# A Strassen-blocked encoder block: where the standard steps stand among a group's phases, shorter leads, and three first sums made by adding transfers

## The chip, the cores and the metric

The kernel runs on one core of a Trainium2 chip. Times are device microseconds (us) of one execution of the whole program; a kernel's time is the median of its runs. One further execution is taken with the hardware profiler, and all rows shown here come from it. The engines are called as the profile calls them: PE (matrix multiplies), DVE (vector), ACT (scalar and activation), POOL (GpSimd) and SP, which here only issues transfers; transfers issued by SP and by POOL go through the core's 16 DMA engines.

## What is computed

One encoder block on 256 frames of 2048 values, all in float32: a half-step SwiGLU feed-forward network, then attention and retention side by side with gates, then a second half-step feed-forward network and a norm.

```python
def swiglu_ffn(x, w_gate, w_up, w_down):
    return (jax.nn.silu(x @ w_gate) * (x @ w_up)) @ w_down
...
x = x + 0.5 * swiglu_ffn(rmsnorm(x, norm_ffn1_g[l]), ffn1_w_gate[l], ffn1_w_up[l], ffn1_w_down[l])
...
x = x + 0.5 * swiglu_ffn(rmsnorm(x, norm_ffn2_g[l]), ffn2_w_gate[l], ffn2_w_up[l], ffn2_w_down[l])
```

`w_gate` and `w_up` are 2048 x 5632, `w_down` is 5632 x 2048. The change touches these two networks alone (named f1 and f2 below); the mixing part between them has the same work in the same order.

## The kernel before

**Products.** Each float32 product is made of three passes: a weight tile `raw` (256 rows x 512 columns, 512 KB, held as 128 x 1024) is split into `hi` by a cast on ACT (L128) and `lo = raw - hi` by a subtraction on DVE (L129), and PE multiplies activations hi with weights hi (L139), activations lo with weights hi (L140) and activations hi with weights lo (L142). A *standard step* takes one such weight tile and both halves of the frames: 12 matmuls of 512 columns.

**Groups.** The 11 blocks of 512 columns of `w_gate` and `w_up` are, but for block 10 (`plain`, standard steps), taken pairwise: one *group* (class `Strassen`, tiles named `z` and a number) multiplies both weights with a Strassen scheme of 7 products in place of 8. A group has four phases. Its steps have 6 matmuls each; they are called `r` (a weight tile as it is) and `s` (a sum of weight tiles), with phase and tile number: `r00` is phase 0, tile 0; `s03` is phase 0, tile 3. In the profile's names `hiz8403s` is the hi part of s03 of group z84. The order in a group is r00 r01 s00 r02 s01 r03 s02 s03, then the same for phases 1 and 2, then s30 to s33: 28 steps. Each network has ten groups.

- Phase 0 needs per tile number a tile `k` of `w_up` and a tile `x` of `w_gate`, loaded by POOL's queue (L542), and the *first sum* x + k. For tiles 0 and 1 DVE makes it (`first`, L531); for tiles 2 and 3 (`ADDED`) POOL issues a transfer that loads `w_up` once more and adds it onto x on the way (L546, `accum_op=ALU.add`). Such a transfer can't be issued before x has landed, and what stands behind it on POOL's queue waits with it.
- Phase 1 loads `raw` tiles by SP; each r step is followed by an addition to x (L593), each s step by k = x - k on DVE (L579) and an adding transfer onto x by POOL (L580, called the *third sum* below).
- Phase 2 loads `raw` tiles by SP and uses k; phase 3 uses x. When the last third sum has been issued, POOL's queue goes on to the loads of the next group's k and x.

Phases 0 (s) and 1 (r) accumulate in one bank, `c`: after s03, ACT takes the sum out (L636), and r10 then writes the bank anew.

**Weaving.** `weave` writes the program's steps in order: a *lead* of standard steps (`LEAD`), then the groups, with standard steps put between pairs of group steps. `SHARE` has 16 numbers, one for each pair of phases 0 to 2 and each single step of phase 3; a standard step is put in when the summed share, times a rate, passes a threshold (lower at a phase's end), and in any case at the end of phase 2. The standard steps are those of block 10, then those of `w_down` for blocks that are ready; each two of the latter are a job whose bank ACT fills and empties (L785, L788). `HELD` and `apart` keep a number of them for the end.

**Look-ahead.** `run` writes, for step c, the splits of up to step c + 3 ahead of c's matmuls (`SPLIT_BUFS` = 4 pairs of hi and lo). So ACT and DVE can be at most four steps ahead of PE, and the cast of a step waits until PE has read the hi of the step four before. SP has 5 `raw` tiles. `kept` are the loads of k and x: for the first group of a network they start 8 steps ahead of the group.

Of the kernel before, what the change touches and what calls it, by code (L numbers as in the profile page):

```python
# [11 lines left out]
ALU = mybir.AluOpType  # L12
# [6 lines left out]
D = 2048  # L19
# [7 lines left out]
NB = 512  # L27
KC = 2
# [7 lines left out]
TAIL = 4  # L36
AHEAD = (2, 3)
HALF_K = D // P // 2
LEAD = 12
MIX_LEAD = 8  # L40
RET_WAIT = (14, 5)
HELD = 6

MIX_SHARE = (0.85,) * 4 + (1.0,) * 4 + (0.8,) + (0.4,) * 3 + (0.15,) * 4
SHARE = (0.7,) * 2 + (0.2,) * 2 + (1.3,) * 4 + (0.3,) * 4 + (0.2,) * 4
ADDED = (2, 3)
PLAIN = 10
PASSES = ((10,),) + tuple((b,) for b in range(10))
GATE_WAIT = 5
# [25 lines left out]
def block_kernel(ctx: ExitStack, tc: tile.TileContext, x, g1, w1g, w1u, w1d, gm, w_in, rel, woa, wor, wo,  # L75
                 g2, w2g, w2u, w2d, gf, cos, sin, decay, ident, out):
    nc = tc.nc
# [19 lines left out]
    def tmp_tile(name, tag="t", bufs=None):  # L97
        return tmp.tile([P, NB], F32, tag=tag, name=name, bufs=bufs)


    steps = []
# [6 lines left out]
    def later(n, fn):  # L108
        due.setdefault(state["step"] + n, []).append(fn)
# [4 lines left out]
    def chunk(w, r0, c0):  # L114
        return w[r0 : r0 + KC * P, c0 : c0 + NB].rearrange("(k p) n -> p k n", p=P)
# [399 lines left out]
    class Strassen:  # L515
# [21 lines left out]
        def loads(self):  # L537


            def go(tiles, i, jc):  # L540
                tiles[jc] = apool.tile([P, KC, NB], F32, tag="act", name=f"{self.name}{'kx'[i]}{jc}")
                nc.gpsimd.dma_start(tiles[jc], chunk(self.w[i], self.rows(0, jc), self.col[i]))  # L542

            def add_on():
                for jc in self.added:
                    nc.gpsimd.dma_start(self.x[jc], chunk(self.w[0], self.rows(0, jc), self.col[0]), accum_op=ALU.add)  # L546

            out = [
                lambda tiles=tiles, i=i, jc=jc: go(tiles, i, jc)
                for jc in range(HALF_K // KC) for i, tiles in enumerate((self.kept, self.x))  # L550
            ]
            out[-1] = lambda last=out[-1]: [last(), add_on()]
            return out

        def steps(self):

# [103 lines left out]
    def down_done(b, factor, after):  # L660
        def done(acc):
            for t in range(NT):
                xb = xs[t][:, b * NB : (b + 1) * NB]
                nc.vector.scalar_tensor_tensor(xb, acc[t], factor, xb, op0=ALU.mult, op1=ALU.add)
            if after is not None:
                after(b)

        return done
# [11 lines left out]
    def weave(jobs, apart, groups, lead, share, start=None):  # L680


        queue = [(job, k) for job in jobs for k in range(0, job.nk, KC)]
        at_hand = {}

        def next_standard():

            if len(queue) <= apart:
                return False
            job, k = queue[0]  # L690
            if any(at_hand.get(b, len(steps) + 1) > len(steps) for b in job.needs):
                return False
            steps.append(standard(job, k))
            del queue[0]
            if job.makes is not None and k + KC == job.nk:
                at_hand[job.makes] = len(steps) + 6
            return True

        for _ in range(lead):
            next_standard()  # L700
        rate = (len(queue) - apart) / (len(groups) * sum(share))
        credit = 0.0
        first = len(steps) - 8
        for n, (b, make) in enumerate(groups.items()):
            group = make()
            loads = group.loads()
            if start is not None and n == 0:
                loads[0] = lambda load=loads[0]: [start(), load()]
            kept.extend((first + i if n == 0 else 0, fn) for i, fn in enumerate(loads))
            for i, part in enumerate(group.steps()):  # L710
                steps.extend(part)
                credit += rate * share[i]
                if i + 1 == len(share):
                    at_hand[b] = len(steps) + 7

                turn = i + 1 == 3 * (HALF_K // KC)
                if (turn or credit >= (0.2 if (i + 1) % (HALF_K // KC) == 0 else 0.6)) and next_standard():
                    credit -= 1
        for job, k in queue:
            steps.append(standard(job, k))  # L720

    def ffn(name, norm, wg, wu, wd, after, start=None):


        nblocks = DFF // NB
        mids, ready = {}, {}

        def put_mid(b, hs):
            mids[b] = Operand(f"{name}a{b}", 1)
            for t in range(NT):  # L730
                mids[b].put(0, t, hs[t])

        def plain(b):
            gates = {}

            wait = GATE_WAIT if start is not None and b == PLAIN else 0

            def gate_done(acc):
                def go():
                    for t in range(NT):  # L740
                        gates[t] = tmp_tile(f"{name}g{b}{t}", "gate", 2)
                        nc.scalar.activation(gates[t], acc[t], AF.Silu, scale=norm.scale(t))

                if wait:
                    later(wait, go)
                else:
                    go()

            def up_done(acc):
                for t in range(NT):  # L750
                    a = gates[t]
                    nc.vector.scalar_tensor_tensor(a, acc[t], norm.scale(t), a, op0=ALU.mult, op1=ALU.mult)  # L752
                later(4, lambda: put_mid(b, gates))

            tags = ("acc", "acc")
            up = Gemm(wu, 0, b * NB, D // P, norm, up_done, tags)
            up.makes = b
            return [Gemm(wg, 0, b * NB, D // P, norm, gate_done, ("z", "z") if wait else tags), up]

        def paired(b):  # L760
            got = {}

            def evict(t, side, r):
                if side == 1:
                    nc.scalar.activation(r, r, AF.Silu)
                    got[t] = r
                    return
                nc.vector.scalar_tensor_tensor(got[t], r, norm.scale(t), got[t], op0=ALU.mult, op1=ALU.mult)
                if t == 1:
                    later(4, lambda: put_mid(b, got))  # L770

            return Strassen(norm, wu, b * NB, wg, b * NB, evict, ADDED)

        def down(blocks, last):

            jobs = []

            def act(k, t):
                return mids[blocks[k // 4]](k % 4, t)

            for b in range(D // NB):
                cols = slice(b * NB, (b + 1) * NB)

                def seed(acc, t, cols=cols):
                    nc.scalar.activation(acc, xs[t][:, cols], AF.Copy, scale=2.0)  # L785

                def evict(acc, t, cols=cols):
                    nc.scalar.activation(xs[t][:, cols], acc, AF.Copy, scale=0.5)  # L788

                if last:  # L790
                    job = Gemm(wd, 0, b * NB, 4 * len(blocks), act, down_done(b, 0.5, after))
                else:
                    job = Gemm(wd, 0, b * NB, 4 * len(blocks), act, None, ("acc", "acc"), seed)
                    job.evict = evict
                job.rows = [(m * 4 + i) * P for m in blocks for i in range(4)]
                job.needs = blocks
                jobs.append(job)
            return jobs

        downs = {blocks: down(blocks, blocks is PASSES[-1]) for blocks in PASSES}  # L800
        jobs = plain(PLAIN) + [job for p in PASSES for job in downs[p]]
        for job, follow in zip(jobs, jobs[1:]):
            job.next = follow
        groups = {b: (lambda b=b: paired(b)) for b in range(nblocks) if b != PLAIN}
        weave(jobs, len(downs[PASSES[-1]]) * len(PASSES[-1]) * 4 // KC + HELD, groups, LEAD, SHARE, start)


    n1 = Norm("n1", gains[:, 0, :], True)
# [221 lines left out]
    def gates(col1, col2, func, dsts):  # L1030


        def evict(t, side, r):
            if side == 1:
                nc.scalar.activation(r, r, func)
            else:
                bank, r = r, tmp_tile(f"sg{col1}{t}", "gate", 2)
                nc.scalar.activation(r, bank, func, scale=nm.scale(t))
            nc.scalar.dma_start(dsts[side][:, t, :], r)

        return Strassen(nm, w_in0, col1, w_in0, col2, evict)

    both = ("acc", "acc")
    groups = {
        b: (lambda b=b: gates(GA + b * NB, GG + b * NB, AF.Sigmoid, merge_dram[b])) for b in range(D // NB)
    }
# [219 lines left out]
```

## Time and profile before

| | |
|---|---|
| time, median of 3 runs | 2078.74 us (2076.82 to 2080.69) |
| the profiled execution's own time | 2079.74 us |
| its span, first to last instruction | 2078.0 us |
| PE busy, weight loads busy | 99%, 81% |
| DVE, ACT, POOL busy | 85%, 72%, 16% |
| transfers by SP's queue (q1), by POOL's (q0) | 301.50 MB, 189.44 MB |
| granted PE clock | 0.999 |

A row of a list of groups gives busy time and mean duration, then idle time before and what ended it. A row of a timeline gives start, duration, engine, line, operation, what is written and read, and in brackets the engine's idle time just before and what ended it. Matmuls are pipelined: a 512-column matmul is shown as 0.39 us long while the next one starts 0.23 us after it, so PE is shown busy for 0.16 us of every wait, and a short wait isn't shown as one. PE's idle time is therefore read here from starts and from counts of instructions.

### The profile page before, as it was taken

The page shows a single profiled execution, that of the slowest core. Times are in us where ns is not written, and L with a number is a line of the kernel's source. Part 1 is how long each engine was busy: PE and PEld are TensorE (multiplying, and loading weights), DVE is VectorE, ACT ScalarE, POOL GpSimd, SP SyncE. Part 2 cuts the span into 40 slices and gives each one's busy share as a digit, 9 for nine tenths or more (in the row PEclk, how much of TensorE's full clock was granted, in tenths as well). Part 3 has the DMA queues.
Part 4 walks back from the last instruction along what each step waited for, and adds up shares of the span by engine and source line. Part 5 has one row for each costly group of instructions (what it writes and reads, how often), then busy time and mean ns, then how long its engine had stood idle before and what let it go on. Part 6 is the DMA issues. An engine that isn't in the chain of part 4 may idle for free. (4 is left out here: it accounts for less than half of the span.)

```text
span 2078.0 us, 26280 instructions
## 1 busy us (share of the span) xinstructions
PE 2047.3 (99%) x9208; PEld 1680.7 (81%) x9208; DVE 1768.2 (85%) x1836; ACT 1490.7 (72%) x1892; POOL 342.3 (16%) x386
## 2 busy tenths in 40 slices
PE   9999999999999999999999999999999999999998
PEld 7777888877888888888888888887878888778877
DVE  7898999989998799899966667568889999889996
ACT  8677888777887767776665434556788787778775
POOL 2221222221122110122100000011122222122210
PEclk9999999999999999999999999999999999999999
DMA  9778889887888777798775645577789888889974
GB/s 325 228 211 247 259 264 289 256 236 226 251 261 251 243 206 258 260 289 252 224 271 174 223 144 189 185 253 181 244 255 291 267 237 231 251 251 272 298 208 132
DMA packets 230325, 498.47 MB, mean 240 GB/s; under 512 B 15584, under 2 KB 16336, under 8 KB 230192
## 3 DMA queue, kind: packets, MB, share of 16 engines
q1 hardware_dynamic: 156736, 301.50, 42.9%
q0 software_dynamic: 70112, 189.44, 35.7%
q10 hardware_dynamic: 3344, 5.84, 0.8%
q8 instruction: 72, 1.18, 0.2%
q14 instruction: 61, 0.50, 0.1%
HBM read 487.81 MB, written 8.91 MB: 239 GB/s over the span
## 5 line engine op out<-in xcount | busy, mean ns | idle before, releaser
L129 DVE TENSOR_TENSOR lo<-raw,hi 128x1024 fp32r<-128x1024 f32 x367 | 447.8, 1224 | 163.4 <-ACT hi L128 161.1
L128 ACT CAST hi<-raw 128x1024 fp32r<-128x1024 f32 x367 | 384.0, 1050 | 206.4 <-PE acc L140 140.0
L788 ACT ACTIVATE xall<-acc 128x512 f32<-128x512 f32 x160 | 94.5, 591 | 17.6 <-PE acc L142 13.1
L785 ACT ACTIVATE acc<-xall 128x512 f32<-128x512 f32 x160 | 95.8, 599 | 15.2 <-DVE f1g L752 7.0
L139 PE MATMUL acc<-hi,mgh 128*128 128x512 f32 x128 | 50.2, 392 | 0.0
L140 PE MATMUL acc<-hi,mgl 128*128 128x512 f32 x128 | 49.8, 389 | 0.0
L139 PE MATMUL acc<-hi,nma01h 128*128 128x512 f32 x96 | 38.6, 403 | 0.0
L139 PE MATMUL acc<-hi,nma00h 128*128 128x512 f32 x96 | 38.6, 402 | 0.0
L140 PE MATMUL acc<-hi,nma00l 128*128 128x512 f32 x96 | 37.5, 390 | 0.0
L139 PE MATMUL acc<-hi,nma10h 128*128 128x512 f32 x96 | 37.5, 390 | 0.0
L140 PE MATMUL acc<-hi,nma01l 128*128 128x512 f32 x96 | 37.5, 390 | 0.0
L140 PE MATMUL acc<-hi,nma11l 128*128 128x512 f32 x96 | 37.4, 390 | 0.0
L139 PE MATMUL acc<-hi,nma11h 128*128 128x512 f32 x96 | 37.4, 390 | 0.0
L140 PE MATMUL acc<-hi,nma10l 128*128 128x512 f32 x96 | 37.4, 390 | 0.0
L142 PE MATMUL acc<-lo,mgh 128*128 128x512 f32 x128 | 35.5, 389 | 0.0
L142 PE MATMUL acc<-lo,nma01h 128*128 128x512 f32 x96 | 29.6, 390 | 0.0
L142 PE MATMUL acc<-lo,nma00h 128*128 128x512 f32 x96 | 29.6, 389 | 0.0
L142 PE MATMUL acc<-lo,nma11h 128*128 128x512 f32 x96 | 29.6, 389 | 0.0
L142 PE MATMUL acc<-lo,nma10h 128*128 128x512 f32 x96 | 29.6, 389 | 0.0
L142 PEld LDWEIGHTS acc<-lo,mgh 128*128 128x128 f32 x128 | 24.0, 188 | 5.0
L140 PEld LDWEIGHTS acc<-hi,mgl 128*128 128x128 f32 x128 | 24.0, 188 | 4.9
L139 PEld LDWEIGHTS acc<-hi,mgh 128*128 128x128 f32 x128 | 24.0, 188 | 4.8
(6634 smaller groups left out, 7144.1 us busy)
## 6 DMA issues: line engine op xcount, KB each, us to landing
raw<-in_ffn_w_down_dram SPq DMA_DIRECT2D x176, 512.0 KB, 6.6
raw<-in_w_in_dram SPq DMA_DIRECT2D x96, 512.0 KB, 4.7
raw<-in_w_out_dram SPq DMA_DIRECT2D x32, 512.0 KB, 4.4
raw<-in_ffn_w_up_dram SPq DMA_DIRECT2D x16, 512.0 KB, 10.3
raw<-in_w_out_att_dram SPq DMA_DIRECT2D x16, 512.0 KB, 4.2
raw<-in_w_out_ret_dram SPq DMA_DIRECT2D x16, 512.0 KB, 4.1
raw<-in_ffn_w_gate_dram SPq DMA_DIRECT2D x15, 512.0 KB, 5.1
z392x<-in_w_in_dram POOLq DMA_DIRECT2D x8, 512.0 KB, 7.5
```

Of the source, the lines that this page charges most:

```text
L128: nc.scalar.copy(hi, raw)
L129: nc.vector.tensor_sub(lo, raw, hi.bitcast(F32))
L139: nc.tensor.matmul(acc, ahi, whi, start=first, stop=False, **more)
L140: nc.tensor.matmul(acc, alo, whi, start=False, stop=False, **more)
L142: nc.tensor.matmul(acc, ahi, wlo, start=False, stop=last, **more)
L785: nc.scalar.activation(acc, xs[t][:, cols], AF.Copy, scale=2.0)
L788: nc.scalar.activation(xs[t][:, cols], acc, AF.Copy, scale=0.5)
```

## The change

Four things change, all in the two feed-forward networks:

- `SHARE` has large numbers in phases 0 and 1, zero in phase 2. The number of standard steps stays the same.
- The lead is 10 standard steps in f1 and 8 in f2, in place of 12. The first group's loads are not staged ahead of step 4.
- First sums 1, 2 and 3 are adding transfers; DVE makes number 0 alone.
- The adding transfer of tile n is issued right behind the load of x of tile n + 1, and that of tile 3 last, where before both stood behind all loads.

```diff
-LEAD = 12
+LEAD = (10, 8)
...
-SHARE = (0.7,) * 2 + (0.2,) * 2 + (1.3,) * 4 + (0.3,) * 4 + (0.2,) * 4
-ADDED = (2, 3)
+SHARE = (0.75,) * 4 + (1.0,) * 4 + (0.0,) * 4 + (0.2,) * 4
+ADDED = (1, 2, 3)
...
-            def add_on():
-                for jc in self.added:
-                    nc.gpsimd.dma_start(self.x[jc], chunk(self.w[0], self.rows(0, jc), self.col[0]), accum_op=ALU.add)
-
-            out = [
-                lambda tiles=tiles, i=i, jc=jc: go(tiles, i, jc)
-                for jc in range(HALF_K // KC) for i, tiles in enumerate((self.kept, self.x))
+            def add_on(jc):
+                nc.gpsimd.dma_start(self.x[jc], chunk(self.w[0], self.rows(0, jc), self.col[0]), accum_op=ALU.add)
+
+            def both(jc):
+                go(self.x, 1, jc)
+                if jc - 1 in self.added:
+                    add_on(jc - 1)
+                if jc + 1 == HALF_K // KC and jc in self.added:
+                    add_on(jc)
+
+            return [
+                (lambda jc=jc: both(jc)) if i else (lambda jc=jc: go(self.kept, 0, jc))
+                for jc in range(HALF_K // KC) for i in range(2)
             ]
-            out[-1] = lambda last=out[-1]: [last(), add_on()]
-            return out
...
-        first = len(steps) - 8
+        first = max(len(steps) - 8, D // NB)
...
-        weave(jobs, len(downs[PASSES[-1]]) * len(PASSES[-1]) * 4 // KC + HELD, groups, LEAD, SHARE, start)
+        weave(jobs, len(downs[PASSES[-1]]) * len(PASSES[-1]) * 4 // KC + HELD, groups, LEAD[start is None], SHARE, start)
```

Written out, the order of a middle group, with `+` for a standard step, goes from (z191) `r00 r01 + s00 r02 s01 r03 s02 s03 + r10 r11 + s10 r12 + s11 r13 + s12 s13 + r20 r21 s20 r22 s21 r23 + s22 s23 + s30 s31 s32 s33`, or (z120) `r00 r01 s00 r02 + s01 r03 s02 s03 r10 r11 + s10 r12 + s11 r13 + s12 s13 + r20 r21 + s20 r22 s21 r23 s22 s23 + s30 s31 s32 s33 +`, to the same in all groups of f1 but the first: `r00 r01 + s00 r02 s01 r03 + s02 s03 + r10 r11 + s10 r12 + s11 r13 + s12 s13 + r20 r21 s20 r22 s21 r23 s22 s23 + s30 s31 s32 s33`. In f2 some groups have `r00 r01 s00 r02 + s01 r03 + s02 s03 +` in its place.

On PE, at the end of phase 0 of the third group of f1 (named z84 before and z82 now; the number is that of the step at which the group begins), this stood before:

```order
L140 MATMUL z84c_1641<-hiz8403s_1690,n1s5l_291 128x512
L139 MATMUL z84c_1641<-hiz8403s_1690,n1s5h_290 128x512
L140 MATMUL z84c_1641<-hiz8403s_1690,n1s5l_291 128x512
L142 MATMUL z84c_1641<-loz8403s_1691,n1s5h_290 128x512 x2
L139 MATMUL z84c_1641<-hiz8410r_1700,n1s3h_474 128x512
L140 MATMUL z84c_1641<-hiz8410r_1700,n1s3l_475 128x512
```

Here s03's last product is followed at once by r10's first, in the same bank. At the same place now:

```order
L142 MATMUL z82c_1615<-loz8203s_1661,n1s5h_290 128x512 x2
L139 MATMUL acc14_0_1690<-hi92_1672,f1a0h0_1098 128x512
L140 MATMUL acc14_0_1690<-hi92_1672,f1a0l0_1099 128x512
L139 MATMUL acc14_0_1690<-hi92_1672,f1a0h0_1098 128x512
L140 MATMUL acc14_0_1690<-hi92_1672,f1a0l0_1099 128x512
L142 MATMUL acc14_0_1690<-lo92_1673,f1a0h0_1098 128x512 x2
L139 MATMUL acc15_1_1693<-hi92_1672,f1a0h0_1098 128x512
L140 MATMUL acc15_1_1693<-hi92_1672,f1a0l0_1099 128x512
L139 MATMUL acc15_1_1693<-hi92_1672,f1a0h0_1098 128x512
L140 MATMUL acc15_1_1693<-hi92_1672,f1a0l0_1099 128x512
L142 MATMUL acc15_1_1693<-lo92_1673,f1a0h0_1098 128x512 x2
L139 MATMUL z82c_1615<-hiz8210r_1696,n1s3h_473 128x512
```

A whole standard step of `w_down` (banks acc) has moved between the two.

On POOL, the loads and adding transfers of the fifth group's first sums (z156 before) stood like this; `k0` is tile 0 of k:

```order
L542 DMA z156k0_2458<-in_ffn1_w_up_dram 128x2x512
L542 DMA z156x0_2484<-in_ffn1_w_gate_dram 128x2x512
L542 DMA z156k1_2520<-in_ffn1_w_up_dram 128x2x512
L542 DMA z156x1_2532<-in_ffn1_w_gate_dram 128x2x512
L542 DMA z156k2_2556<-in_ffn1_w_up_dram 128x2x512
L542 DMA z156x2_2568<-in_ffn1_w_gate_dram 128x2x512
L542 DMA z156k3_2583<-in_ffn1_w_up_dram 128x2x512
L542 DMA z156x3_2601<-in_ffn1_w_gate_dram 128x2x512
L546 DMA z156x2_2568<-in_ffn1_w_up_dram 128x2x512
L546 DMA z156x3_2601<-in_ffn1_w_up_dram 128x2x512
```

And now (the same group is z154, the adding transfers are L545):

```order
L542 DMA z154k0_2440<-in_ffn1_w_up_dram 128x2x512
L542 DMA z154x0_2471<-in_ffn1_w_gate_dram 128x2x512
L542 DMA z154k1_2496<-in_ffn1_w_up_dram 128x2x512
L542 DMA z154x1_2508<-in_ffn1_w_gate_dram 128x2x512
L542 DMA z154k2_2532<-in_ffn1_w_up_dram 128x2x512
L542 DMA z154x2_2544<-in_ffn1_w_gate_dram 128x2x512
L545 DMA z154x1_2508<-in_ffn1_w_up_dram 128x2x512
L542 DMA z154k3_2560<-in_ffn1_w_up_dram 128x2x512
L542 DMA z154x3_2584<-in_ffn1_w_gate_dram 128x2x512
L545 DMA z154x2_2544<-in_ffn1_w_up_dram 128x2x512
L545 DMA z154x3_2584<-in_ffn1_w_up_dram 128x2x512
```

There is one adding transfer more, and k3 and x3 now stand behind the first of them, which waits for x1.

## The prediction

> **What bounds the kernel now.** I read the page's busy times first, then PE's waits, then windows of whole groups, and last the timelines of POOL, DVE and ACT over one group.
>
> ```profile
> PE 2047.3 (99%) x9208; PEld 1680.7 (81%) x9208; DVE 1768.2 (85%) x1836; ACT 1490.7 (72%) x1892; POOL 342.3 (16%) x386
> ```
>
> PE is the bound, and the change leaves its matmuls as they are. So only PE's waits can come or go. By name they are small (total, times, longest):
>
> ```profile
> PE z84c L139 <- ACT z84s L636: 0.8, 1, 0.8
> PE z263c L142 <- DVE loz26300s L129: 0.6, 1, 0.6
> ```
>
> Since ends of matmuls are modelled, waits are better counted. The next rows are stretches of the two networks: us, then busy time and count of PE, PEld, DVE, ACT, POOL, then PE clock, DMA share, GB/s.
>
> ```profile
> 110.90:274.60 163.70, 160.47 (x710) 130.18 (x709) 152.37 (x140) 127.49 (x157) 35.04 (x39) 1.00 0.83 237
> 274.60:396.00 121.40, 121.40 (x545) 100.72 (x544) 113.01 (x105) 98.69 (x121) 25.57 (x29) 1.00 0.89 259
> 396.00:640.00 244.00, 239.97 (x1063) 195.66 (x1063) 221.38 (x204) 191.33 (x233) 49.10 (x53) 1.00 0.86 252
> 1412.40:1447.50 35.10, 34.57 (x154) 27.73 (x153) 31.04 (x29) 21.71 (x25) 3.58 (x3) 1.00 0.60 156
> 1447.50:2007.00 559.50, 551.92 (x2443) 450.23 (x2442) 512.30 (x472) 442.47 (x540) 120.91 (x131) 1.00 0.87 255
> ```
>
> The second stretch, two groups long, has PE busy without a gap: 121.40 / 545 = 0.2228 us per PE instruction row. At that pitch the others would take 158.2, 236.8, 34.3 and 544.2 us. They took 5.5, 7.2, 0.8 and 15.3 us more: **28.8 us of waits**, the most that the new placing can win there. The clock is 1.00 throughout. A group at full pitch takes 60.7 us (two in 121.4).
>
> What nearly bounds as well is a loop through POOL. This is POOL in group z191, in the stretch without a gap (start, duration, idle before):
>
> ```profile
> 332.82 1.23 POOL L542 DMA_DIRECT2D z191k<-in_ffn_w_up_dram  x1
> 337.19 1.20 POOL L542 DMA_DIRECT2D z191k<-in_ffn_w_up_dram  x1
> 342.04 0.73 POOL L542 DMA_DIRECT2D z191x<-in_ffn_w_gate_dram  x1 [3.65 <-issue]
> 354.88 1.23 POOL L546 DMA_DIRECT2D z191x<-in_ffn_w_up_dram  x1 [12.11 <-DMA z191x<-in_ffn_w_gate_dram]
> 359.04 1.21 POOL L546 DMA_DIRECT2D z191x<-in_ffn_w_up_dram  x1 [2.93 <-DVE z191x L531]
> 392.82 1.19 POOL L580 DMA_DIRECT2D z191x<-in_ffn_w_up_dram  x1 [1.09 <-ACT hiz19120r L128]
> 393.55 1.23 POOL L542 DMA_DIRECT2D z227k<-in_ffn_w_up_dram  x1
> ```
>
> And ACT's cast of s03, which needs the last adding transfer, with DVE from there to the last addition of phase 1:
>
> ```profile
> 366.74 1.05 ACT L128 CAST hiz19103s<-z191x 128x1024 fp32r<-128x1024 f32 x1 [0.58 <-DVE loz19102s L129]
> 367.82 1.22 DVE L129 TENSOR_TENSOR loz19103s<-z191x,hiz19103s 128x1024 fp32r<-128x1024 f32 x1
> 370.61 1.22 DVE L129 TENSOR_TENSOR loz19110r<-rawz19110r,hiz19110r 128x1024 fp32r<-128x1024 f32 x1 [0.43 <-ACT hiz19110r L128]
> 371.75 1.22 DVE L593 TENSOR_TENSOR z191x<-z191x,rawz19110r 128x1024 f32<-128x1024 f32 x1
> 391.05 1.23 DVE L579 TENSOR_TENSOR z191k<-z191x,z191k 128x1024 f32<-128x1024 f32 x1
> ```
>
> The loop: k0 is issued at 332.82; s03 is cast at 366.74, **33.9 us** later; then DVE works through phase 1 back to back (only the 0.43 us of idle is spare), the last third sum is issued at 392.82, and the next k0 at 393.55. From the cast to there are 26.8 us, without the idle 26.4. Period 60.7: exactly a group of PE's. So a first leg of 60.7 − 26.4 = 34.3 us is free, and z191 uses 33.9. That is possible to use up, because z191 has just three standard steps (8.2 us of PE) between the preceding r20 and s02; so had z156, z335, z840, z875 and z1019, where others had four.
>
> **The change part by part.** *Placing.* Each group now has a standard step between s03 and r10, and phases 1 and 2 as z191 has them, including six steps of phase 2 without a standard one, which cost z191 no wait. PE's waits for ACT L636 (the bank's emptying, now behind 2.72 us of other work) and for the lo of s00 (a standard step now precedes it, as in z191) go. I take 28 of the 28.8 us, leaving 0.8 for stray ones: **−28**. Cover: the standard steps; where it fails, the 0.8 us of the row above comes back at each of 18 boundaries. What becomes late next is the loop above, since by the written order fifteen groups (all but the first two of f1, and z728, z801, z837, z873, z910, z982, z1018 of f2) now have three standard steps before s02.
>
> *Leads.* The first group of f1 loses its start either way:
>
> ```profile
> 44.70:110.90 66.20, 63.02 (x274) 49.83 (x273) 58.35 (x62) 47.49 (x59) 13.81 (x15) 1.00 0.83 238
> ```
>
> 274 rows at 0.2228 are 61.0 us; 5.2 are waits for loads and splits just begun. Ten lead steps leave 5.4 us less time for them and then find more standard steps inside the group; between −5 and +5, I take 0, as PE work and loads both keep their sums. f2's lead likewise.
>
> *First sum 1 by transfer.* DVE loses this, 20 times in all (busy total and mean of one):
>
> ```profile
> L531 DVE TENSOR_TENSOR z191x<-z191x,z191k 128x1024 f32<-128x1024 f32 x2 | 2.4, 1222 | 0.0
> ```
>
> That is 24.4 us of DVE, but in phase 0, where the leg waits for transfers; so no gain on the path. POOL's 20 added issues of 1.2 us are hidden while it waits. The price is paid in the 16 DMA engines: do they have room in the leg?
>
> ```profile
> 340.00:357.00 17.00, 17.00 (x77) 14.08 (x76) 14.32 (x14) 14.40 (x18) 1.96 (x2) 1.00 1.03 388
> 367.00:371.00 4.00, 4.00 (x19) 3.31 (x18) 3.57 (x5) 3.71 (x5) 0.00 (x0) 1.00 0.00 0
> 1976.00:1979.00 3.00, 3.00 (x15) 2.46 (x14) 2.00 (x3) 1.52 (x3) 0.00 (x0) 1.00 1.02 164
> ```
>
> They are full (1.03) while the loads run, at 388 GB/s, and idle only after s03's transfer is in. The last row is a lone adding transfer (of z1019, below): the engines are as full (1.02), but move 164 GB/s. 512 KB (524 thousand bytes) at 164 GB/s take **3.2 us**, against 1.35 at 388. Put into a full leg, that makes 33.9 + 3.2 = 37.1, 2.8 over 34.3.
>
> The Trainium skill ("DMA: Bandwidth & Descriptors", section "Anatomy of one DMA — SWDGE (gpsimd) path") gives one price for each transfer issued by GpSimd, about 2.0 us fixed plus bytes over 436 GB/s; the fixed part being mostly a wait for the write's receipt, the engines would by it be taken for 1.2 us (an estimate), added or plain. The trace's plain loads come near that with 388 GB/s, its adding transfer doesn't.
>
> *The order.* The adding transfer of x1 waits for x1, and k3 and x3 now stand behind it. Issue to landing of the four k tiles:
>
> ```profile
> DMA to landing us min/median/max: 10.4/14.7/19.2
> ```
>
> k0 landed at 343.2 (the least, 10.4) and k3 at 356.4 (the greatest, from 337.19), six tiles later: 2.2 us each, so x1 at 349.8. Half a microsecond more to the transfer's issue, 0.7 for each issue (steps of the rows above): x3 goes out at 351.8, 19 us after k0, where it went at 342.04, 9.2 after. z1019 has this delay by chance, since four transfers of `gf` came between its loads:
>
> ```profile
> 1943.26 1.23 POOL L542 DMA_DIRECT2D z1019k<-in_ffn_w_up_dram  x1
> 1945.46 2.65 POOL L1209 DMA_DIRECT2D gf<-in_norm_final_g_dram  x4
> 1959.82 0.72 POOL L542 DMA_DIRECT2D z1019x<-in_ffn_w_gate_dram  x1 [0.38 <-issue]
> 1974.16 1.21 POOL L546 DMA_DIRECT2D z1019x<-in_ffn_w_up_dram  x1 [3.72 <-DVE z983c L768]
> 1980.15 1.05 ACT L128 CAST hiz101903s<-z1019x 128x1024 fp32r<-128x1024 f32 x1 [0.65 <-DMA z1019x<-in_ffn_w_up_dram]
> ...
> PE z1019c L139 <- ACT hiz101903s L128: 0.5, 1, 0.5
> ```
>
> x3 went out 16.6 us after k0, and s03's cast came at 36.9, waiting for the transfer, with PE behind it. Two estimates agree; I take the seen one, 36.9: **36.9 + 26.4 = 63.3, 2.6 us over a group of PE's**, 14 times = 36.4. Bounds: nothing, if the lost delay and the added bytes fit where other loads give way; and 5.0: x3 sent at 351.8, landing as in z1019 13.9 us later, 0.5 to the issue, 5.9 to the cast there, makes 372.1, a leg of 39.3. In the fifteenth, z1018, `gf` comes as well: 36.9 + 3.2 − 34.3 = 5.8.
>
> Sum: 36.4 + 5.8 − 28 = **+14.2**. The profiled execution took 2079.74 us; that gives 2093.9. The median of the runs is 1.0 lower: **2093 us**.
>
> **The rivals.**
>
> *Hidden transfers (the other side).* The engines' order lets the added transfer through in time: raw tiles of SP, which share the engines and are wanted later than s02 and s03, give way. For it: at 367 the engines go idle, and 0.89 of DMA share over the clean groups leaves 6.7 us per group. Against: the share is full in just the leg that counts, and z1019's wait. It decides where the leg stays under 34.3, that is 0.4 us over z191's. Then −28, and z1018 unharmed: 2051.
>
> *The price of a plain transfer.* If the adding transfer costs what a load costs where others run beside it, the leg is 33.9 + 1.35 = 35.25, 0.95 over: 14 × 0.95 = 13.3, z1018 about 3: −28 + 16 = −12, **2067**. The Trainium skill's single price for both kinds, named above, leads here. For it: the 164 GB/s are those of a transfer with no other beside it. Against: the engines' time was full with it.
>
> *Even.* At 1.7 us a group, 23.8 + 4.9 − 28 is about 0: 2079; 1.4 to 1.9 gives this, between the last one and the forecast.
>
> *Serial.* Each transfer behind x1 waits out the one before, 5.0 per group: 70 + 8.2 − 28 = +50, 2129.
>
> That the change does not do what it says is no case: the written order shows the standard steps behind s03, and the third adding transfer ahead of k3.
>
> **How the numbers follow.** Forecast (1.9 to 3.4 us a group: 2082 to 2105) 0.44; hidden 0.17; plain price 0.17; even 0.12; serial 0.10. About 0.2%, 4 us, is what a measurement can tell from no change. Faster by more: the hidden and plain cases and a third of even, 0.38. Slower by more: forecast and serial, 0.54. Within: 0.08. For 8 in 10 the range leaves out a good half of hidden and most of serial: 2054 to 2116. The forecast's own range is 2082 to 2105.
>
> **What would show it.** Right: PE's waits for ACT L636 and for the lo of s00 are gone from the list; x3 is issued about 19 us after k0, s03's cast comes 36 to 37 us after k0 and waits for DMA, PE waits at s03 in most groups, and groups follow each other at 63 us. Wrong: k0 to cast under 34.3 and groups at 60.7 us (hidden), or near 35 and 61.6 (plain price). The idle stretch of DMA after s03 should shrink or go. Placing is wrong if waits for ACT L636 stay, or if phase 2 now waits for hi or lo.

## The result and the profile after

| | before | after |
|---|---|---|
| time, median of 4 runs | 2079.31 us (2076.82 to 2080.69) | 2116.66 us (2114.3 to 2117.24) |
| ratio | | 1.0179, 95% interval 1.0166 to 1.0192 |
| span of the profiled execution | 2078.0 us | 2115.5 us |

The change makes the kernel 37 us slower. The direction was forecast (+14 us), the size was not: 2117 lies above the range, which ended at 2116. PE has its waits in the profile now; the page's busy times of the changed kernel:

```profile
PE 2068.1 (98%) x9208; PEld 1680.9 (79%) x9208; DVE 1747.0 (83%) x1816; ACT 1483.7 (70%) x1892; POOL 367.7 (17%) x406
```

Counts of PE and ACT are the same; DVE has 20 instructions less and POOL 20 more, as written. The stretches of the two networks in the changed kernel, by columns as before:

```profile
112.00:668.00 556.00, 537.78 (x2327) 426.61 (x2327) 475.58 (x437) 413.64 (x514) 119.88 (x125) 1.00 0.87 246
1468.90:2046.00 577.10, 566.03 (x2473) 455.37 (x2471) 503.76 (x464) 441.61 (x545) 128.79 (x137) 0.99 0.89 257
```

At the clean pitch of 0.2228 us a row these would take 518.3 and 550.9 us. So 37.7 us are lost in f1 and 26.2 in f2, where the kernel before lost 12.7 and 15.3 in the matching stretches, by the prediction's rows (5.5 + 7.2 in f1, 15.3 in f2). PE's list of waits in the changed kernel names two kinds:

```profile
PE z154c L139 <- ACT hiz15403s L128: 3.4, 1, 3.4
...
PE z226c L139 <- ACT hiz22603s L128: 1.4, 1, 1.4
...
PE z226c L139 <- ACT z226s L640: 1.1, 1, 1.1
```

The first kind was forecast: s03 is late. The second was to be gone: L640 is the old L636, the emptying of bank c, and r10 still waits for it, though a standard step of 2.72 us now stands in between. POOL in z226 of the changed kernel, the first to the last load of its phase 0:

```profile
409.64 1.23 POOL L542 DMA_DIRECT2D z226k<-in_ffn_w_up_dram  x1
...
428.66 1.23 POOL L545 DMA_DIRECT2D z226x<-in_ffn_w_up_dram  x1 [14.16 <-DMA z226x<-in_ffn_w_gate_dram]
...
430.15 1.23 POOL L542 DMA_DIRECT2D z226x<-in_ffn_w_gate_dram  x1
...
439.86 1.22 POOL L545 DMA_DIRECT2D z226x<-in_ffn_w_up_dram  x1 [6.09 <-DMA z226x<-in_ffn_w_gate_dram]
```

And ACT in the same group, from the cast of s03 to the emptying of bank c:

```profile
446.93 1.04 ACT L128 CAST hiz22603s<-z226x 128x1024 fp32r<-128x1024 f32 x1 [2.88 <-DMA z226x<-in_ffn_w_up_dram]
...
448.39 1.04 ACT L128 CAST hi<-raw 128x1024 fp32r<-128x1024 f32 x1
449.34 0.59 ACT L789 ACTIVATE acc<-xall 128x512 f32<-128x512 f32 x1
449.87 0.57 ACT L792 ACTIVATE xall<-acc 128x512 f32<-128x512 f32 x1
450.48 0.60 ACT L789 ACTIVATE acc<-xall 128x512 f32<-128x512 f32 x1
451.01 0.58 ACT L792 ACTIVATE xall<-acc 128x512 f32<-128x512 f32 x1
451.49 1.04 ACT L128 CAST hiz22610r<-rawz22610r 128x1024 fp32r<-128x1024 f32 x1
452.43 1.04 ACT L128 CAST hiz22611r<-rawz22611r 128x1024 fp32r<-128x1024 f32 x1
453.38 0.69 ACT L640 ACTIVATE z226s<-z226c,n1minus 128x512 f32<-128x512 f32 x1
```

x3 goes out 20.5 us after k0 (forecast 19), and s03's cast comes 37.3 us after k0 and waits for DMA (forecast 36 to 37): that leg is as worked out. Over all twenty groups the leg is 32.0 to 41.2 us, 36.5 in the middle. Behind it stands something that the prediction did not have: four copies between banks and `xall` (L789, L792), 2.15 us from 449.34 to 451.49. They fill and empty the bank of a job of two standard steps. Here one job ends and the next begins right at the standard step behind s03. So r10's cast and the emptying of bank c come 2.15 us later.

### The profile page after: what moved, and what is told of

The parts are those of the page before. It is cut to its first block, busy times and chain, and to the rows that moved or that the text cites. A ratio compares the mean times of both kernels' runs of the same rounds, so it can differ in the third digit from the quotient of the medians.

```text
span 2115.5 us, 26308 instructions
## 1 busy us (share of the span) xinstructions
PE 2068.1 (98%) x9208; PEld 1680.9 (79%) x9208; DVE 1747.0 (83%) x1816; ACT 1483.7 (70%) x1892; POOL 367.7 (17%) x406
## 4 chain that ended last, share of the span: by engine, by line
PE 68%; DMA 15%; issue 7%; ACT 5%; POOL 2%; DVE 2%; ACTq 0%; DVEq 0%; POOLq 0%
PE acc L142 13%; PE acc L139 12%; PE acc L140 12%; DMA z262x<-in_ffn_w_gate_dram 1%; DMA z226x<-in_ffn_w_gate_dram 1%; DMA z982x<-in_ffn_w_gate_dram 1%; DMA z10x<-in_ffn_w_gate_dram 1%; DVE lo L129 1%; ACT xall L792 1%; ACT hi L128 1%; DMA z1018k<-in_ffn_w_up_dram 1%; DMA z801x<-in_ffn_w_gate_dram 1%; DMA z946x<-in_ffn_w_gate_dram 1%; DMA z910x<-in_ffn_w_gate_dram 0%; DMA z154x<-in_ffn_w_gate_dram 0%
## 5 line engine op out<-in xcount | busy, mean ns | idle before, releaser
L792 ACT ACTIVATE xall<-acc 128x512 f32<-128x512 f32 x160 | 94.1, 588 | 18.0 <-PE acc L142 15.7
L789 ACT ACTIVATE acc<-xall 128x512 f32<-128x512 f32 x160 | 95.8, 599 | 8.5 <-DVE f1g L756 4.5
L140 PE MATMUL acc<-hi,nma01l 128*128 128x512 f32 x96 | 37.5, 390 | 0.0
L140 PE MATMUL acc<-hi,nma00l 128*128 128x512 f32 x96 | 37.5, 390 | 0.0
```

Source lines behind the costliest of these rows:

```text
L140: nc.tensor.matmul(acc, alo, whi, start=False, stop=False, **more)
```

## The experiments

Each time is a median, with the ratio to the kernel before measured beside it; the kernel before had 2077.75, 2077.55 and 2078.55 us in the three sets (the first four rows, the next four, the last two).

| kernel | us | ratio, 95% interval |
|---|---|---|
| new places and leads, two adding transfers | 2077.76 | 1.0001 (0.9992 to 1.0010) |
| old places and leads, three adding transfers between the loads | 2118.85 | 1.0195 (1.0175 to 1.0215) |
| old places and leads, three adding transfers behind the loads | 2098.54 | 1.0097 (1.0080 to 1.0115) |
| new places alone | 2081.49 | 1.0016 (1.0006 to 1.0026) |
| changed kernel, plain transfers for adding ones | 2063.69 | 0.9929 (0.9914 to 0.9943) |
| changed kernel, f1's jobs shifted by a step | 2104.97 | 1.0122 (1.0102 to 1.0142) |
| new places, two adding transfers, f1's jobs shifted | 2063.05 | 0.9926 (0.9911 to 0.9941) |
| changed kernel, adding transfers behind the loads | 2109.02 | 1.0147 (1.0132 to 1.0162) |
| the seventh, one adding transfer | 2061.38 | 0.9920 (0.9903 to 0.9936) |
| the seventh, f2's jobs shifted too | 2061.59 | 0.9919 (0.9904 to 0.9933) |

**1. The change without its third adding transfer.**

```diff
-ADDED = (1, 2, 3)
+ADDED = (2, 3)
```

> The changed kernel with two adding transfers again (tiles 2 and 3, behind all loads; DVE makes first sums 0 and 1); its places of the standard steps and its leads stay, so PE's order is that of the changed kernel. Theory A (the third adding transfer and its place make s03 late; the waits for the bank's emptying and for later splits are its follow-ons): s03's cast comes about 34 us after k0's issue, groups follow at 60.7 to 61.5 us, time 2050 to 2062 us. Theory B (the new places themselves cost: three standard steps before s02 are too few, and the exchange of banks between jobs falls behind s03): PE still waits at r10 for the bank in most groups, time 2095 to 2115 us.

2077.76 us: neither. Without the third transfer the 39 us are gone, so they are the price of the transfer and of its place together (this kernel's two stand behind all loads); but the 16 us or more that theory A still counted on do not come, and the new places and leads by themselves are worth nothing. Where did the waits go that they remove? Stretches of both networks in this kernel:

```profile
106.00:640.00 534.00, 527.84 (x2329) 428.23 (x2328) 484.02 (x446) 416.67 (x512) 109.84 (x117) 1.00 0.86 248
1442.70:2002.00 559.30, 553.90 (x2464) 453.75 (x2463) 509.78 (x471) 441.64 (x543) 116.35 (x127) 1.00 0.88 255
```

At the clean pitch these are 518.8 and 548.9 us: 15.2 us lost in f1, where it was 12.7, and 10.4 in f2, where it was 15.3. In PE's waits the old ones for the bank of c and for the lo of s00 are gone in most groups. This stands in their place:

```profile
PE acc L142 <- DVE lo L129: 6.3, 13, 0.6
...
PE z1018c L139 <- ACT hiz101803s L128: 1.4, 1, 1.4
...
PE z1018c L139 <- ACT z1018s L640: 1.1, 1, 1.1
```

The first of these in the kernel before:

```profile
PE acc L142 <- DVE lo L129: 1.7, 5, 0.6
```

Most of the new ones are in f1, at the standard step after r01. This is what stands ahead of it on ACT, in z226 of this kernel:

```profile
408.96 1.04 ACT L128 CAST hiz19032s<-z190x 128x1024 fp32r<-128x1024 f32 x1
409.90 0.60 ACT L789 ACTIVATE acc<-xall 128x512 f32<-128x512 f32 x1
410.43 0.59 ACT L792 ACTIVATE xall<-acc 128x512 f32<-128x512 f32 x1
411.05 0.60 ACT L789 ACTIVATE acc<-xall 128x512 f32<-128x512 f32 x1
411.59 0.58 ACT L792 ACTIVATE xall<-acc 128x512 f32<-128x512 f32 x1
412.07 1.04 ACT L128 CAST hiz19033s<-z190x 128x1024 fp32r<-128x1024 f32 x1
```

and behind it on DVE:

```profile
413.14 1.23 DVE L129 TENSOR_TENSOR loz19033s<-z190x,hiz19033s 128x1024 fp32r<-128x1024 f32 x1 [1.88 <-ACT hiz19033s L128]
...
416.02 1.22 DVE L531 TENSOR_TENSOR z226x<-z226x,z226k 128x1024 f32<-128x1024 f32 x1
...
418.30 1.22 DVE L531 TENSOR_TENSOR z226x<-z226x,z226k 128x1024 f32<-128x1024 f32 x1
419.43 1.22 DVE L129 TENSOR_TENSOR lo<-raw,hi 128x1024 fp32r<-128x1024 f32 x1
```

The same four copies, at the end of a group, hold up the cast of s33; DVE waits 1.88 us for it and then has two first sums among its splits, and has not caught up at the standard step's lo. The copies behind s03 cost in this kernel too: from the cast of s03 to the next k0 it takes 28.6 us (428.55 to 457.13 in z226), where 26.4 were free, and with z226's leg of 33.1 that is 61.7, over a group of PE's. Which of the two places costs how much was not separated. Why in each group? With a lead of 10, ten groups share 80 standard steps, eight each. That is an even number, so the jobs of two keep their place from the second group of f1 to the last.

**2. The third adding transfer in the old order.** The table's second kernel takes the new `loads` and the three adding transfers (old shares, leads of 12), the third only the number, for which this is the edit:

```diff
-ADDED = (2, 3)
+ADDED = (1, 2, 3)
```

> The kernel before with only its first sums changed: three adding transfers, placed between the loads as in the changed kernel; places and leads as before. Theory A: groups with four standard steps before s02 have 2.7 us of slack and lose little, the five or six with three lose 3 to 5 us each, so slower: 2085 to 2105 us. Theory B: as before within 4 us, 2075 to 2083.

> The kernel before with a third adding transfer (tile 1), all three behind all loads; nothing else changed. If the time of the added transfer in the DMA engines is what makes s03 late, nearly as slow as with the transfers between the loads: 2083 to 2100 us. If it is the late issue of k3 and x3 behind the wait for x1, no slower than before: 2075 to 2082. Theory B: 2075 to 2083.

2118.85 and 2098.54 us. Between the loads the third transfer costs 41 us in the old order too, where I expected at most 27: groups with four standard steps ahead of s02 are hit as well (PE waits 1.5 us for z84's s03 and 1.6 us for z299's there). Behind all loads it costs 21. So in the old order half is the transfer itself, and half its place between the loads; that the wait for x1 ahead of k3 and x3 is what costs there is the likely reading.

**3. The places alone.**

```diff
-SHARE = (0.7,) * 2 + (0.2,) * 2 + (1.3,) * 4 + (0.3,) * 4 + (0.2,) * 4
+SHARE = (0.75,) * 4 + (1.0,) * 4 + (0.0,) * 4 + (0.2,) * 4
```

> The kernel before with only the new shares; leads of 12 and two adding transfers stay, so that some groups get four standard steps before s02 and two have none between s03 and r10. Theory A: PE's waits at s00 and r10 go, 2050 to 2064 us. Theory B: 2085 to 2110 us.

2081.49 us, slower by 1 to 5 us in the interval: neither theory again. It agrees with the first experiment that the new places win nothing.

**4. Adding transfers at the price of plain ones.** This kernel leaves out the first sums of tiles 1 to 3.

```diff
-nc.gpsimd.dma_start(self.x[jc], chunk(...), accum_op=ALU.add)
+nc.gpsimd.dma_start(self.x[jc], chunk(...))
```

> The changed kernel, but the three transfers that add load the same bytes over x in place of adding them (so the sums x + k of tiles 1 to 3 are left out); order and waits stay. Theory P (an adding transfer holds the 16 DMA engines for 3.2 us, a plain one for 1.35, and this price is what is lost): 5.5 us less in each leg, s03's cast 33 us or less after k0's issue, time near that of the kernel with two adding transfers, 2065 to 2085 us. Theory Q (what is lost is the late issue of k3 and x3 behind x1's landing): cast still 36 us after k0, time 2100 to 2118 us.

2063.69 us, 53 us below the changed kernel and a little better than theory P had it. The written order, and what each transfer must wait for, are those of the changed kernel; this is z226's leg in this kernel, first on POOL:

```profile
390.54 1.22 POOL L542 DMA_DIRECT2D z226k<-in_ffn_w_up_dram  x1
...
410.69 0.72 POOL L542 DMA_DIRECT2D z226x<-in_ffn_w_gate_dram  x1
...
418.98 0.72 POOL L545 DMA_DIRECT2D z226x<-in_ffn_w_up_dram  x1 [5.12 <-DMA z226x<-in_ffn_w_gate_dram]
```

then the cast of s03 on ACT:

```profile
423.10 1.05 ACT L128 CAST hiz22603s<-z226x 128x1024 fp32r<-128x1024 f32 x1 [1.38 <-DMA z226x<-in_ffn_w_up_dram]
```

x3 is sent out 20.2 us after k0, as late as in the changed kernel (20.5); but the last transfer goes out at 28.4 in place of 30.2, and s03's cast at 423.10 is 32.6 us after k0 in place of 37.3. So the late issue alone does not bring the leg over the free 34.3 us; only with the time that adding takes in the engines does it. The single price of the Trainium skill for a GpSimd transfer ("DMA: Bandwidth & Descriptors", "Anatomy of one DMA — SWDGE (gpsimd) path") does not hold for adding here: the same bytes in the same places cost 53 us more when added.

It also beats the two-transfer kernel by 14 us. Two things can be behind this. DVE has one first sum where that one has two, and PE's waits for the lo of a standard step are nearly gone from its list:

```profile
PE acc L142 <- DVE lo L129: 0.3, 1, 0.3
```

against 6.3 us in the first experiment. And the leg is shorter, 32.6 us in z226 against 33.1. No run separates the two, so what a sum taken off DVE is worth by itself is not shown.

**5. The jobs shifted.** One standard step more in f1's lead, one less kept for its end: from the second group on, the steps of f1 stand in the same order, but each job begins one step earlier. Once with three adding transfers, once with two:

```diff
-LEAD = (10, 8)
+LEAD = (11, 8)
...
-        weave(jobs, len(downs[PASSES[-1]]) * len(PASSES[-1]) * 4 // KC + HELD, groups, ...)
+        weave(jobs, len(downs[PASSES[-1]]) * len(PASSES[-1]) * 4 // KC + HELD - (start is not None), groups, ...)
```

> The changed kernel with 11 lead steps in f1 and one standard step less kept for f1's end, so that from its second group on f1 has the same order of steps, but each job of two standard steps begins one place earlier. Theory J (ACT's four bank copies between two jobs, 2.2 us, stand behind the cast of s03 and ahead of r10's, and so make r10 wait for the emptying of bank c): PE's waits at r10 in f1, 1.3 us in each of eight groups with about 1.3 us of follow-ons, go; 10 to 20 us faster than the changed kernel, 2097 to 2107 us. Theory K (r10 waits because s03 itself is late; the copies only fill time): as the changed kernel within 5 us, 2111 to 2121.

> The kernel with two adding transfers and the new places, with the jobs of f1 shifted by one standard step in the same way. There PE waits 0.8 us for the lo of the standard step after r01 in nearly each group of f1. Theory J (ACT's copies between two jobs stand in phase 3 ahead of the casts of s33, r00 and r01): these waits go and no others come, 8 to 15 us faster: 2062 to 2070 us. Theory D (DVE has too much to do there: two first sums among four splits): the waits stay, 2074 to 2082 us.

2104.97 and 2063.05 us, 11.7 and 14.7 us less than without the shift: theory J in both. With two adding transfers, f1 now runs without a gap from r20 of its second group to r20 of its ninth, seven groups; the row is of the second of these kernels:

```profile
149.80:576.00 426.20, 426.20 (x1906) 352.38 (x1905) 395.97 (x365) 343.50 (x421) 91.66 (x100) 1.00 0.90 259
```

These seven groups took 437.2 us in the first experiment:

```profile
147.00:584.20 437.20, 432.12 (x1905) 350.41 (x1904) 395.53 (x364) 341.81 (x421) 91.31 (x99) 1.00 0.88 253
```

They take 60.9 us each now, 62.5 there. ACT's copies now stand behind the cast of s01:

```profile
415.25 1.06 ACT L128 CAST hiz22701s<-z227x 128x1024 fp32r<-128x1024 f32 x1 [0.30 <-PE z227a L140]
416.20 0.59 ACT L789 ACTIVATE acc<-xall 128x512 f32<-128x512 f32 x1
...
418.38 0.60 ACT L792 ACTIVATE xall<-acc 128x512 f32<-128x512 f32 x1
418.87 1.05 ACT L128 CAST hiz22703r<-z227k 128x1024 fp32r<-128x1024 f32 x1
```

This kernel is faster than the changed one, by 53.6 us, and than the kernel before, by 14.5.

**6. All adding transfers behind the loads, in the new order.**

```diff
-                if jc - 1 in self.added:
-                    add_on(jc - 1)
-                if jc + 1 == HALF_K // KC and jc in self.added:
-                    add_on(jc)
+                if jc + 1 == HALF_K // KC:
+                    for late in self.added:
+                        add_on(late)
```

> The changed kernel with all three adding transfers behind all loads. With the added transfer's time in the DMA engines alone, some 20 us over the kernel with two adding transfers, as it was in the old places: 2092 to 2103 us. If the place between the loads costs nothing in the new order of steps: 2111 to 2120.

2109.02 us, between the two expectations: 7.6 us below the changed kernel, 31 over two transfers. PE's waits hint at why the old place wins less here than its 20 us in the old order. Some have moved from s03 to s01, whose sum is now a transfer that is issued late:

```profile
PE z154c L139 <- ACT hiz15401s L128: 1.7, 1, 1.7
...
PE z82c L139 <- ACT hiz8201s L128: 1.3, 1, 1.3
```

**7. Two variants of the best.** One adding transfer (`ADDED = (3,)`), and f2's jobs shifted as well (a lead of 9, `HELD = 5`):

> The kernel with the new places and f1's jobs shifted, but one adding transfer (tile 3) and three first sums on DVE. If the leg through the DMA engines still bounds any group there, another transfer of 3.2 us less makes it faster: 2055 to 2061 us. If two transfers fit the leg, nothing is won and DVE's third sum among the splits of phase 0 costs up to 0.8 us in each of 18 groups: 2063 to 2078 us.

> The kernel with two adding transfers and the new places, jobs shifted by one standard step in f1 and in f2 alike. Theory J (the place of ACT's copies between two jobs decides): f2's groups had little to win, as PE waits 5 us in all in its eight middle groups; moving the copies to the bad place in the groups where they stood well costs 0.8 to 1.3 us each: 2061 to 2073 us. A gain below 2061 us would mean that the shift helps by something else than the place of the copies.

2061.38 and 2061.59 us, ratios 0.9920 and 0.9919 against 0.9926: neither can be told from the seventh kernel. With one adding transfer the time lies just above the first range expected and below the second: neither a shorter leg nor DVE's third sum shows. So two adding transfers fit the leg once the copies stand well, as far as this tells, and f2 has nothing to gain from a shift, as theory J had it.

## Why the prediction had the direction and missed the size

*What bounds the kernel.* Right: PE's work stayed, and what it loses in the two networks' stretches grew from 28.0 us to 63.9, which is 36 of the span's 37.5. But not all of it is waiting. The four longest of PE's waits in the two networks (1.7 to 5.2 us) are each followed by a stretch at a granted clock of 0.50, which the prediction, with a clock of 1.00 throughout, did not have. These are two stretches of the changed kernel behind the wait of 3.4 us for z154's s03 (PE's count and busy time, then clock, DMA share, GB/s at the end):

```profile
320.00:323.00 3.00, 3.00 (x8) 2.34 (x8) 1.14 (x2) 2.97 (x6) 0.00 (x0) 0.50 0.30 86
325.00:328.00 3.00, 3.00 (x15) 2.38 (x13) 3.00 (x4) 3.00 (x5) 0.00 (x0) 1.00 0.55 163
```

Taken in slices of 1 us, the missing part of the clock times PE's busy time makes some 7 us in all (an estimate); the kernel before and the first experiment's have no such stretch while PE works.

*The leg through POOL.* Right. x3 was forecast 19 us after k0, the cast 36.9; z226 has 20.5 and 37.3. The second part of the loop, 26.4 us from the cast to the next k0, holds where ACT's copies stand elsewhere (26.8 us from z801's cast to the next k0, as in z191), and is 2.15 us longer in f1, where they stand behind s03.

*The third adding transfer, +42.2 us.* Right in sum: 38.9 in the new order (2116.66 less 2077.76), 41.1 in the old one. That the sum is so near is in part luck, since how it is spread was not right, and the 7 us at a clock of 0.50 are in it. These are seven groups of f1 and eight of f2 in the changed kernel, each from r20 to r20:

```profile
150.00:608.50 458.50, 441.96 (x1905) 349.43 (x1904) 389.82 (x358) 339.69 (x421) 100.42 (x107) 1.00 0.88 249
1468.90:1978.50 509.60, 502.73 (x2210) 406.62 (x2209) 450.12 (x415) 394.27 (x487) 114.50 (x121) 1.00 0.90 258
```

A group of f2 takes 63.7 us, 3.0 over the clean 60.7 where 2.6 were forecast; one of f1 takes 65.5, which is 4.8 over, and 2.15 of that are ACT's copies behind s03 in the second part of the loop. Against the first experiment, which has these copies in the same places, a group of f1 takes 3.0 us more (62.5 there) and one of f2 only 1.6 (62.1, by the row below), so the forecast of one price for fourteen groups was not right:

```profile
1442.70:1939.60 496.90, 494.97 (x2209) 407.32 (x2208) 457.54 (x423) 396.26 (x487) 104.50 (x113) 1.00 0.89 256
```

The sum taken off DVE, which I put at nothing, may win back some of the waits at the standard step after r01 (3.6 us in the changed kernel's list, 6.3 in the first experiment's); that was not separated.

*Placing and leads, −28 us.* This is the step that failed: "I take 28 of the 28.8 us, leaving 0.8 for stray ones". It measured 0 (2077.76 against 2077.75): the new places alone cost 3.7 us, and the leads, put at 0 between −5 and +5, won 3.7 (2081.49 to 2077.76). The sentence before it, that phases 1 and 2 stand "as z191 has them", looked at the order of steps on PE, and that was true. But a standard step is not only its matmuls. Each second one brings four copies on ACT. The kernel before has them here around z191 (two of the places, the first of the four copies in each):

```profile
342.23 0.59 ACT L785 ACTIVATE acc<-xall 128x512 f32<-128x512 f32 x1
...
360.54 0.59 ACT L785 ACTIVATE acc<-xall 128x512 f32<-128x512 f32 x1
```

The first place is ahead of s23, well before the end of the preceding group; the second is 6 us ahead of the cast of s03. In their stead, the new groups of f1 have them ahead of s33 and behind s03. The jobs shifted by one step, with the order of PE unchanged, give 14.7 us of the 28 back. The rest is nearly all in f2. In the kernel with the shift its stretch still loses 11.1 us:

```profile
1430.00:1992.00 562.00, 556.53 (x2473) 455.30 (x2472) 511.87 (x473) 443.93 (x546) 117.50 (x128) 1.00 0.89 255
```

The last group holds some of it: there, as in the first experiment, PE waits for z1018's s03 and its bank (1.4 and 1.1 us shown in the first experiment); that the transfers of `gf` among its loads are the reason was not tested. What the other waits of f2 are due to was not tried.

*The rivals.* Hidden is out: s03 is late in most groups. Even, which put the transfers at 23.8 + 4.9 us and the rest at −28, is out by both: they cost 38.9, and the rest won nothing. The plain price is out by experiment 4: adding is dearer than loading, in a leg full of other transfers too. Serial named 2129 with a leg of 39.3 us; z226's is 37.3, and what brings the total near is the missing gain.

*What would show it wrong* was named: waits for ACT L636 stay. They did, as L640.

## What to carry to other kernels

When a step of work is moved on one engine, list what it brings on the other engines, and how often: here every second standard step carries 2.2 us of ACT's work, and an even number of steps per period fixes that work at one place in every period, good or bad. A gain read from one clean period of the old kernel holds only where all engines' orders agree with it. And a transfer that adds as it lands was paid here in the DMA engines' time: moving a sum of 1.22 us from DVE to it, between the loads, cost 39 us in 20 groups.

## What the runs showed of the hardware

An adding transfer took more of the DMA engines' time here than a plain one of the same bytes, also beside other traffic. The profile's page gives packets, MB and the share of the engines' time for each queue; POOL's is this in the changed kernel (span 2115.5 us) and in experiment 4 (span 2060.4 us):

```profile
q0 software_dynamic: 75552, 199.93, 37.8%
q0 software_dynamic: 67872, 199.93, 34.5%
```

The bytes are the same; 60 transfers add in the first and load in the second. That is 128 packets more for each adding transfer, and 800 against 711 us of the engines' time, or 1.5 us for each (an estimate from these rounded shares; the prediction had 3.2 less 1.35). In the stretch of z226 with adding transfers and loads under way, the changed kernel has its engines full at 286 GB/s (share, GB/s in the last two columns):

```profile
433.00:440.00 7.00, 7.00 (x36) 5.83 (x36) 6.28 (x7) 4.19 (x6) 0.91 (x2) 1.00 1.05 286
```

and nearly the same stretch (23 us behind k0) with plain transfers at 377:

```profile
414.00:419.00 5.00, 5.00 (x27) 4.16 (x26) 5.00 (x6) 3.19 (x4) 0.02 (x1) 1.00 1.01 377
```

After its longest waits PE worked at a granted clock of 0.50 for a while: behind the wait of 3.4 us in z154, 3 us hold 8 PE instructions at a clock of 0.50, and 15 at 1.00 shortly after (the two rows in the part on what bounds the kernel).
